# The adaLN gate of a hybrid attention step, moved from TensorE's query stage to VectorE, GpSimd and ScalarE

## Chip, cores, metric

One core of one Trainium2 chip. The metric is the device time of one execution in microseconds (us), the median of several runs. The engines are named as in the profile: PE is TensorE's matmul queue and PEld its weight loads, DVE is VectorE, ACT ScalarE, POOL GpSimd and SP SyncE, which here only issues DMAs. ACTq and SPq rows are DMA issues of those engines.

## What is computed

One layer of a diffusion backbone, over 128 context tokens and 1024 latent tokens of width 1024. Cut to what matters here:

```
shift, scale, gate = split(silu(cond) @ w_mod + b_mod, 3)      # cond = c for latent tokens, c_ctx for context tokens
h  = rmsnorm(x) * (1 + scale) + shift
p  = h @ w_in             # queries, keys, values and SiLU gates of head groups A (global) and B (windowed)
o_a, o_b = attention of each group
x  = x + gate * (concat(o_a * silu(g_a), o_b * silu(g_b)) @ w_out)
```

The adaLN `gate` is two rows of 1024 numbers, one for each kind of token: `silu(c)` and `silu(c_ctx)` times the last third of `w_mod` (1024 x 1024, 4 MB in f32), plus its part of `b_mod`. Nothing needs it before the output projection, near the middle of the kernel.

## The kernel before

Tokens are 9 tiles of 128 (tile 0 is the context), weights are streamed by blocks of 128 rows. Products with f32 accuracy are made of three passes over parts in a rounded format: `Weights.split` makes a high part on ACT and a low part, the difference, on DVE (L233 to L235). The stages follow each other: modulation with the first gate columns, the SiLU gates of group A, **the query stage**, keys and values, the SiLU gates of group B, attention with the output projection.

The query stage (L551 to L675, pool `qt`) sweeps the 9 token tiles twice: m=0 for the queries of group A, m=1 for those of B. Each tile is one `block` (L267) of 24 products into a PSUM bank, written out in two halves. Before each half `tick()` runs what was put on an agenda with `later(n, f)`, n ticks ahead. Within one tick the agenda runs in the order in which it was filled, and at the end `in_order` ties every engine to the order in which the program was written (L1260). So an instruction that waits holds back all that was written after it for its engine.

For block b the agenda of `query` (L586) holds:

- tick 2b+3, `squares`: squares on ACT (sqq), their sums on DVE (ssq, then ms), a power on POOL (rs, L173);
- tick 2b+5, `scale`: on DVE the scaled queries (qn) and the rotary products (ra, then rb in two parts);
- tick 2b+6, `rotated`: their sum on DVE (qf);
- tick 2b+9, `turned`: four transposes on PE (ptq, L622) into one of two PSUM banks used in turn (`bank_tr`), a copy on ACT (qo0, L625) and its store, issued by ACT (L635);
- tick 2b+10, `low`: the remainder on DVE (qo1, L630), stored by ACT one tick later.

A turning bank is free for block b+2 when qo1 of block b has been taken from it. In the last block of a sweep `split` prepares the weights of the next: `W_QB` at the end of m=0, `W_KV` at the end of m=1. Their raw tiles are loaded by `load_all` (L225) before the last block but one, where the second pair of rotary tables (`rope_tables`, L541) is loaded too; DVE multiplies the tables by the norm gains two ticks later (L546).

The gate is computed by PE in the same stage. Its weights come in four loads of 1 MB into two buffers (`load_wg`, L579); for each half of the columns, `gate_rows` (L569) runs 16 products in four groups of rows at once, ACT copies the bank, and `gate_sum` (L563) adds the four groups with a small product of PE and stores the row in DRAM (`gate_row`), from where it is read back, one row repeated over 128 partitions, before attention (L1055).

Of the kernel before, what the change touches and what calls it, by code (L numbers as in the profile page):

```python
# [9 lines left out]
F32 = mybir.dt.float32  # L10
F32R = mybir.dt.float32r
BF16 = mybir.dt.bfloat16
AF = mybir.ActivationFunctionType
ALU = mybir.AluOpType
# [4 lines left out]
P = 128  # L19
D = 1024  # L20
KT = D // P
# [50 lines left out]
EX_AT = (2, 2, 5)  # L72
ROWS_AT = (1, 1, 4, 6)
KV_ORDER = [0] + list(range(1, NT))
GATE_AT = (3, 7)
QUERY_LAST = (0, 1, 2, 4)
CACHE_AT = 8
VC_AT = 6
# [29 lines left out]
def hybrid_step(ctx, tc, x_prompt, x_sample, cache_k_a, cache_v_a, cache_k_b, cache_v_b,  # L108
# [3 lines left out]
    nc = tc.nc  # L112
# [7 lines left out]
    gate_row = dram.tile([2, D], F32, name="gate_row")  # L120
# [5 lines left out]
    def later(n, f):  # L126

        agenda.setdefault(now[0] + n, []).append(f)
# [26 lines left out]
    ident_r = cst.tile([P, P], F32R, name="ident_r")  # L155
# [45 lines left out]
    silc = sm.tile([P, 16], F32, name="silc")  # L201
# [109 lines left out]
    with tc.tile_pool(name="st", bufs=2, side="right") as st:  # L311
# [29 lines left out]
        sil32 = st.tile([P, KT, 32], F32, name="sil32", bufs=1)  # L341
# [99 lines left out]
        for j in range(KT + 2):  # L441
# [42 lines left out]
            if X_FROM + 1 < j <= X_FROM + 4:  # L484
                t = rest[j - X_FROM - 2]
# [8 lines left out]
            if KT - 2 <= j < KT:  # L494
# [3 lines left out]
                c0, n = W_QA.cols[0]  # L498
# [52 lines left out]
    with tc.tile_pool(name="qt", bufs=2, side="right") as qt:  # L551
        for w in (W_QB, W_KV):
            w.pools = [(qt, KT)] * KT


        sil32 = qt.tile([P, KT, 32], F32, name="sil32g", bufs=1)
        nc.gpsimd.memset(sil32, 0.0)
        nc.vector.tensor_copy(sil32[:, :, 0:2], silc.rearrange("p (c k) -> p k c", c=2))
        sel = qt.tile([P, 2], F32, name="selg", bufs=1)
        group_sum(sel, ident_r.bitcast(F32))  # L560
        wg, bg = [], []

        def gate_sum(n, grow):  # L563
            pgs = bank_tr(f"pgs{n}")
            nc.tensor.matmul(pgs[0:2], sel, grow, start=True, stop=True)
            nc.vector.tensor_tensor(bg[n], pgs[0:2], bg[n], op=ALU.add)
            nc.sync.dma_start(gate_row[:, 512 * n : 512 * n + 512], bg[n])

        def gate_rows(n):  # L569
            pg = bank_mm(f"pgate{n}")  # L570
            for k in range(KT):
                a = 32 * (k % 4)
                nc.tensor.matmul(pg[a : a + 32], sil32[:, k, :], wg[2 * n + k // 4][:, k % 4, :],
                                 start=(k < 4), stop=(k >= 4), tile_position=(0, a))
            grow = qt.tile([P, 512], F32, tag="grow", name=f"grow{n}", bufs=1)
            later(1, lambda: nc.scalar.copy(grow, pg))
            later(3, lambda: gate_sum(n, grow))

        def load_wg(i):  # L579
            n, b = divmod(i, 2)  # L580
            wg.append(qt.tile([P, 4, 512], F32, tag="wg", name=f"wg{i}"))
            nc.sync.dma_start(wg[i], w_mod_g[512 * b : 512 * b + 512, 512 * n : 512 * n + 512].rearrange(
                "(k p) n -> p k n", p=P))


        def query(pq, m, t, tabs, n=1):  # L586

            nm = f"q{m}_{t}"
            pqv = pq.rearrange("p (h d) -> p h d", d=HD)
            v = {}  # L590

            def squares():
                sq = qt.tile([P, 8, HD], F32, tag="sq", name=f"sq{nm}")
                nc.scalar.activation(sq, pqv, AF.Square)  # L594
                ss = qt.tile([P, 8], F32, tag="ss", name=f"ss{nm}")
                nc.vector.tensor_reduce(ss, sq, axis=AX.X, op=ALU.add)
                v["r"] = rsqrt_mean(qt, ss, HD, 8, nm)

            def scale():
                qn = qt.tile([P, 8, HD], F32, tag="qn", name=f"qn{nm}")  # L600
                nc.vector.tensor_tensor(qn, pqv, v["r"].unsqueeze(2).to_broadcast([P, 8, HD]), op=ALU.mult)
                v["qn"] = qn
                if t:
                    v["rot"] = rope_products(qt, qn, 8, *tabs[m], t, nm)

            def rotated():

                qf = qt.tile([P, 4, 2, HD], F32, tag="qf", name=f"qf{nm}", bufs=3)
                out = qf.rearrange("p h g d -> p g h d")
                pair = lambda a: a.rearrange("p (g h) d -> p g h d", g=2)  # L610
                if t:
                    nc.vector.tensor_tensor(out, *(pair(a) for a in v["rot"]), op=ALU.add)
                else:
                    nc.vector.tensor_tensor(
                        out, pair(v["qn"]), gain4[:, 2 * m, :].unsqueeze(1).unsqueeze(1).to_broadcast([P, 2, 4, HD]),
                        op=ALU.mult)
                v["qf"] = qf

            def turned():
                ptq = bank_tr(f"pt{nm}")  # L620
                for h in range(4):
                    nc.tensor.transpose(ptq[:, P * h : P * h + P], v["qf"][:, h].rearrange("p g d -> p (g d)"),  # L622
                                        ident_r.bitcast(F32))
                qo = [qt.tile([P, 512], F32R, tag=f"qo{i}", name=f"qo{i}{nm}") for i in range(2)]
                nc.scalar.copy(qo[0], ptq)  # L625
                put(qo[0], 0)
                later(1, lambda: low(ptq, qo))

            def low(ptq, qo):
                nc.vector.tensor_tensor(qo[1], ptq, qo[0], op=ALU.subtract)  # L630
                later(1, lambda: put(qo[1], 1))

            def put(part, i):
                for g in range(2):
                    nc.scalar.dma_start(q_dram[t][m][64 * i : 64 * i + 64, 512 * g : 512 * g + 512],  # L635
                                       part[64 * g : 64 * g + 64].bitcast(F32))

            for d, f in zip(QUERY_LAST if (m, t) == (1, 0) else QUERY_AT, (squares, scale, rotated, turned)):
                later(n + d, f)

        tabs = {0: rope_tables(qt, 0, 2)}
        for m in range(2):
            w, nxt = ((W_QA, W_QB), (W_QB, W_KV))[m]
            ts = list(range(1, NT)) + [0]
            for t in ts:
                pq = bank_mm(f"pq{m}_{t}")
                if m == 1 and t in (ts[GATE_AT[0]], ts[GATE_AT[1]]):
                    gate_rows(len(wg) // 2 - 1)
                if (m, t) in ((0, ts[-2]), (1, ts[GATE_AT[0]])):
                    n = len(wg) // 2  # L650
                    load_wg(2 * n)
                    load_wg(2 * n + 1)
                    if n == 0:
                        bgt = qt.tile([34, 512], F32, name="bg", bufs=1)
                    bg.append(bgt[32 * n : 32 * n + 2])
                    nc.sync.dma_start(bg[n], b_mod[:, 2 * D + 512 * n : 2 * D + 512 * n + 512].to_broadcast([2, 512]))
                if t == ts[-2]:
                    nxt.load_all()
                    if m == 0:
                        tabs[1] = rope_tables(qt, 2, 2)  # L660
                block(pq, lambda k: project(pq, w, t, k), nxt, t == ts[-1])
                query(pq, m, t, tabs)

        kc = gsw4
        vc = wrp.tile([P, 512], F32, tag="raw", name="vc")[:, 0:256].rearrange("p (m g d) -> p m g d", m=2, g=2)
        for m, (ck, cv) in enumerate(((cache_k_a, cache_v_a), (cache_k_b, cache_v_b))):
            nc.sync.dma_start(kc[:, 2 * m : 2 * m + 2, :], ck[0, 0])
            nc.sync.dma_start(vc[:, m], cv[0, 0])
        pks = []
        for t in KV_ORDER[:AHEAD]:  # L670
            pk = bank_mm(f"pk{t}")
            block(pk, lambda k: project(pk, W_KV, t, k), None, False)
            pks.append(pk)
        while agenda:
            tick()  # L675
# [348 lines left out]
    for i in EARLY:  # L1024
        items, end = max_items(i)
# [260 lines left out]
def _layout(c, c_ctx, norm_gain, b_mod, w_mod):  # L1286

    cols = np.concatenate([a.reshape(-1, P) for a in (c, c_ctx, norm_gain, b_mod)]).T
    w = w_mod[0].reshape(KT, P, 3, KT, P)
    ss = np.stack([w[:, :, 1], w[:, :, 0]], axis=2).transpose(3, 1, 0, 2, 4)  # L1290
    return {"cols": cols, "w_mod_ss": ss, "w_mod_g": w_mod[0][:, 2 * D :]}


# [29 lines left out]
```

## Time and profile before

| | |
|---|---|
| median of 3 runs | 723.17 us (723.15 to 726.25) |
| profiled execution | span 721.3 us; its own device time is not listed apart from the three runs, the median of which is 1.9 us above the span |
| PE busy | 698.3 us, 97% of the span |
| DVE, ACT, POOL busy | 457.6 (63%), 411.7 (57%), 335.3 us (46%) |
| mean granted TensorE clock | 0.993 of full speed |
| DMA | 78.56 MB, mean 109 GB/s |
| query stage, m=0 | from 89.3 to 140.8 us |
| query stage, m=1 | from 140.8 to 201.8 us |

How to read it: shares are averages over stages with different limits. A row of a timeline gives start, length, engine, line, operation, output <- inputs and a count; what stands in brackets is how long the engine was idle before it and what it waited for. A row of the groups gives the count, the busy time, the mean ns of one, and the idle time before.

### The profile page before, as it was taken

To read this page: it belongs to the slowest core of one execution; us is meant where nothing else is said; L and a number is where in the kernel's file an instruction comes from. 1 tells how busy PE (TensorE), PEld (TensorE's weight loads), DVE (VectorE), ACT (ScalarE), POOL (GpSimd) and SP (SyncE) were. 2 spreads that over 40 slices of the span, in tenths; PEclk is the share of its full clock that TensorE was granted. 3 is DMA by queue.
4 is the path that set the end of the run, shared out by engine and by line. 5 is a ranking of instruction groups with operands and counts; after the bars stand their busy time and mean duration, and the time that the engine had idled before them with its cause. 6 is when DMAs were issued, how large, how long until landed. Compare 5 with 4: busy or idle time off the path is not lost. (4 is left out here: it accounts for less than half of the span.)

```text
span 721.3 us, 10622 instructions
## 1 busy us (share of the span) xinstructions
PE 698.3 (97%) x3524; PEld 559.7 (78%) x3524; DVE 457.6 (63%) x1007; ACT 411.7 (57%) x829; POOL 335.3 (46%) x355
## 2 busy tenths in 40 slices
PE   5999999999999999999999999999999999999997
PEld 2678988877777788977788888888888888887865
DVE  3466147875675872745866677577666775775653
ACT  5355411411232451158778877877787778877770
POOL 3456013332322340236666555655575557555751
PEclk9999999999999999999999999999999999999999
DMA  8961373348435115440321222121212221212323
GB/s 344 346 219 59 121 278 86 79 94 276 121 85 142 45 60 171 139 143 23 103 67 45 73 67 88 44 81 52 87 54 59 66 87 45 81 53 87 103 65 119
DMA packets 53159, 78.56 MB, mean 109 GB/s; under 512 B 6569, under 2 KB 25449, under 8 KB 52081
## 3 DMA queue, kind: packets, MB, share of 16 engines
q1 hardware_dynamic: 44928, 65.96, 28.1%
q10 hardware_dynamic: 8176, 11.94, 6.3%
q8 instruction: 28, 0.46, 0.3%
q14 instruction: 27, 0.21, 0.1%
HBM read 58.69 MB, written 19.18 MB: 108 GB/s over the span
## 5 line engine op out<-in xcount | busy, mean ns | idle before, releaser
L1108 POOL TENSOR_TENSOR pl<-pe,ph 128x512 fp32r<-128x512 f32 x130 | 167.6, 1292 | 144.7 <-DVE nm L919 67.5
L859 DVE TENSOR_REDUCE mx<-pmx 128x1 f32<-128x384 f32 x192 | 101.4, 552 | 59.5 <-PE pmx L858 58.1
L1100 ACT ACTIVATE pe<-st 128x512 f32<-128x512 f32 x146 | 86.8, 594 | 28.0 <-PE st L1098 27.1
L1104 ACT CAST ph<-pe 128x512 fp32r<-128x512 f32 x146 | 90.6, 621 | 4.8
L1118 PE MATMUL pv<-ph,v_hi 128*128 128x512 f32 x208 | 83.2, 400 | 2.2 <-DVE spare L1142 2.2
L1121 PE MATMUL pv<-pl,v_hi 128*128 128x512 f32 x208 | 82.6, 397 | 0.0
L173 POOL TENSOR_TENSOR rs_q<-ms_q,mhalf 128x8 f32<-128x8 f32 x18 | 34.8, 1931 | 82.1 <-DVE ms_q L171 82.1
L1189 PE MATMUL po<-wo,ogh 128*128 128x512 f32 x216 | 72.5, 394 | 0.2 <-DVE yt L1196 0.2
L919 DVE CUSTOM_DVE_ANT_0 sn<-sn,mask,nsink 128x512 f32<-128x512 f32 (+1 forms) x64 | 46.3, 724 | 38.3 <-PE sn L916 36.5
L858 PE MATMUL pmx<-kha,qt 128*128 128x384 f32 x192 | 61.0, 363 | 0.4 <-ACT pen L905 0.2
L1097 PE MATMUL st<-qt,kha 128*128 128x512 f32 x144 | 58.3, 405 | 1.5 <-ACT pe L1100 0.8
L1098 PE MATMUL st<-qb,kla 68*128 68x512 f32 x144 | 57.6, 400 | 1.1 <-DVE qb L878 1.1
L1120 PE MATMUL pv<-ph,v_lo 128*64 128x512 f32 x146 | 57.9, 396 | 0.0
L1121 PEld LDWEIGHTS pv<-pl,v_hi 128*128 128x128 f32 x208 | 39.4, 189 | 16.7 <-issue 0.2
L905 ACT ACTIVATE pen<-sn,nm 128x512 f32<-128x512 f32 (+2 forms) x72 | 45.0, 626 | 6.5 <-DVE nm L919 3.1
L1093 ACT CAST ph<-st 128x512 fp32r<-128x512 f32 x62 | 36.4, 587 | 19.9 <-PE st L1092 18.7
L1118 PEld LDWEIGHTS pv<-ph,v_hi 128*128 128x128 f32 x208 | 39.4, 189 | 10.5 <-ACT ogh L1154 2.4
L1189 PEld LDWEIGHTS po<-wo,ogh 128*128 128x128 f32 x216 | 40.0, 188 | 6.8 <-DVE yt L1196 0.6
L1094 DVE TENSOR_TENSOR pl<-st,ph 128x512 fp32r<-128x512 f32 x62 | 42.5, 686 | 2.3 <-ACT ph L1093 1.5
L1189 PE MATMUL po<-wo,ogl 128*128 128x512 f32 x108 | 42.6, 394 | 0.0
L594 ACT ACTIVATE sqq<-pq 128x512 f32<-128x512 f32 x18 | 10.8, 599 | 53.3 <-DMA qd<-qo0q 14.4
L858 PEld LDWEIGHTS pmx<-kha,qt 128*128 128x128 f32 x192 | 35.5, 190 | 6.2 <-DVE mx L859 1.4
(216 smaller groups left out, 1700.2 us busy)
## 6 DMA issues: line engine op xcount, KB each, us to landing
qt<-qd SPq DMA_DIRECT2D x36, 256.0 KB, 3.1
wm<-in_w_mod_ss_dram SPq DMA_DIRECT2D x8, 1024.0 KB, 5.1
qd<-qo0q ACTq DMA_DIRECT2D x36, 128.0 KB, 2.4
qd<-qo1q ACTq DMA_DIRECT2D x36, 128.0 KB, 2.4
sgl<-gd SPq DMA_DIRECT2D x36, 128.0 KB, 2.1
out_dram<-yt SPq DMA_DIRECT2D x17, 256.0 KB, 2.1
xn<-in_x_sample_dram SPq DMA_DIRECT2D x8, 512.0 KB, 7.0
wg<-in_w_mod_g_dram SPq DMA_DIRECT2D x4, 1024.0 KB, 7.9
```

The costliest lines, as they stand in the source:

```text
L858: nc.tensor.matmul(pm[:, 0:384], lhs, kha[:, g, 3 * b : 3 * b + 3, :], start=True, stop=True)
L859: nc.vector.tensor_reduce(mx[:, h, b : b + 1], pm[:, 0:384], axis=AX.X, op=ALU.max)
L919: nc.vector.tensor_tensor_reduce(s, s, mask[:, m0 : m0 + n], -1.0, nsink[:, 4 * g + h : 4 * g + h + 1], op0=ALU.add, op1=ALU.min, accum_ou ...
L1097: nc.tensor.matmul(s, kh, qtile[i], start=True, stop=False)
L1098: nc.tensor.matmul(s, kl, qbtile[i], start=False, stop=True)
L1100: nc.scalar.activation(pe, s, AF.Exp)
L1104: nc.scalar.copy(ph, pe)
L1108: nc.gpsimd.tensor_tensor(pl, pe, ph, op=ALU.subtract)
L1118: nc.tensor.matmul(pv, two, ph, start=(b == 0), stop=False)
L1120: nc.tensor.matmul(pv[0:64, :], vl, ph, start=False, stop=False)
L1121: nc.tensor.matmul(pv, two, pl, start=False, stop=last)
L1189: nc.tensor.matmul(po[n], a, wo_parts[KT * n + k][lo], start=(k == KS[0] and p == 0), stop=(k == KS[-1] and p == 2))
```

## The change

The gate's products and sums leave PE. The host hands over the gate's third of `w_mod` transposed, with `c` and `c_ctx` as two more rows. A column of the gate is then a sum along the free dimension: for each of 8 groups of 128 columns a tile of transposed weights (128 x 1024) is multiplied by the SiLU of `c_ctx` on POOL and summed by an accumulating copy on ACT, and multiplied by the SiLU of `c` and summed in one instruction on DVE. The 16 columns get their bias, are turned by one transpose on PE, and go to `gate_row` as before.

The two condition rows are repeated over the partitions (`silb`, 2 x 512 KB written) and loaded at the head of the stage, ahead of the first rotary tables, together with the first two weight tiles. The weights now come in 8 loads of 512 KB through two buffers; each later load follows, one tick on, the sum that frees its buffer. Column group j is begun at tick 6 + 3j (`GATE_AT`), its sums are at the tick after that, the bias at tick 30 and the transpose at tick 31.

```diff
-GATE_AT = (3, 7)
+GATE_AT = (6, 3)
...
-        sil32 = qt.tile([P, KT, 32], F32, name="sil32g", bufs=1)
-        nc.gpsimd.memset(sil32, 0.0)
-        nc.vector.tensor_copy(sil32[:, :, 0:2], silc.rearrange("p (c k) -> p k c", c=2))
-        sel = qt.tile([P, 2], F32, name="selg", bufs=1)
-        group_sum(sel, ident_r.bitcast(F32))
-        wg, bg = [], []
-        def gate_sum(n, grow):
...
-        def gate_rows(n):
...
+        silb = qt.tile([P, 2, D], F32, name="silb", bufs=1)
+        gcol = qt.tile([P, 2, KT], F32, name="gcol", bufs=1)
+        gbias = qt.tile([P, KT], F32, name="gbias", bufs=1)
+        for c in range(2):
+            nc.sync.dma_start(silb[:, c], w_mod_g[D + c : D + c + 1, :].to_broadcast([P, D]))
+        nc.sync.dma_start(gbias, cols[:, 40:48])
+        wg = {}
+        def load_wg(j):
+            wg[j] = qt.tile([P, D], F32, tag="wg", name=f"wg{j}")
+            nc.sync.dma_start(wg[j], w_mod_g[P * j : P * j + P, :])
+        def gate_silu(c):
+            nc.scalar.activation(silb[:, c], silb[:, c], AF.Silu)
+        def gate_columns(j):
+            prod = qt.tile([P, D], F32, tag="prod", name=f"prod{j}", bufs=1)
+            nc.gpsimd.tensor_tensor(prod, wg[j], silb[:, 1], op=ALU.mult)
+            def summed():
+                nc.scalar.activation(prod, prod, AF.Copy, accum_out=gcol[:, 1, j : j + 1])
+                w = wg.pop(j)
+                nc.vector.tensor_tensor_reduce(w, w, silb[:, 0], 1.0, 0.0, op0=ALU.mult, op1=ALU.add,
+                                               accum_out=gcol[:, 0, j : j + 1])
+                if j + 2 < KT:
+                    later(1, lambda: load_wg(j + 2))
+            later(1, summed)
+        def gate_turned():
+            pt = bank_tr("ptg")
+            nc.tensor.transpose(pt[0:16, 0:P], gcol.rearrange("p c j -> p (c j)"), ident_r.bitcast(F32))
+            grow = qt.tile([16, P], F32, name="grow", bufs=1)
+            nc.scalar.copy(grow, pt[0:16, 0:P])
+            nc.sync.dma_start(gate_row.rearrange("c (j n) -> (c j) n", n=P), grow)
+        for j in range(2):
+            load_wg(j)
+            later(3 + j, lambda j=j: gate_silu(j))
+        for j in range(KT):
+            later(GATE_AT[0] + GATE_AT[1] * j, lambda j=j: gate_columns(j))
+        end = GATE_AT[0] + GATE_AT[1] * KT
+        later(end, lambda: nc.vector.tensor_tensor(gcol, gcol, gbias.unsqueeze(1).to_broadcast([P, 2, KT]), op=ALU.add))
+        later(end + 1, gate_turned)
...
-                if m == 1 and t in (ts[GATE_AT[0]], ts[GATE_AT[1]]):
-                    gate_rows(len(wg) // 2 - 1)
-                if (m, t) in ((0, ts[-2]), (1, ts[GATE_AT[0]])):
-                    n = len(wg) // 2
-                    load_wg(2 * n)
-                    load_wg(2 * n + 1)
...
-    return {"cols": cols, "w_mod_ss": ss, "w_mod_g": w_mod[0][:, 2 * D :]}
+    return {"cols": cols, "w_mod_ss": ss, "w_mod_g": np.concatenate([w_mod[0][:, 2 * D :].T, c.reshape(1, D), c_ctx.reshape(1, D)])}
```

More of the change, by code (lines that the diff above doesn't have):

```diff
@@ L553, in hybrid_step @@
             w.pools = [(qt, KT)] * KT
-        sil32 = qt.tile([P, KT, 32], F32, name="sil32g", bufs=1)
-        nc.gpsimd.memset(sil32, 0.0)
-        nc.vector.tensor_copy(sil32[:, :, 0:2], silc.rearrange("p (c k) -> p k c", c=2))
-        sel = qt.tile([P, 2], F32, name="selg", bufs=1)
-        group_sum(sel, ident_r.bitcast(F32))
-        wg, bg = [], []
-        def gate_sum(n, grow):
[L564 to L567, printed above, removed]
@@ L569, in gate_rows @@
-        def gate_rows(n):
[L570 to L583, printed above, removed]
+        silb = qt.tile([P, 2, D], F32, name="silb", bufs=1)
[3 more added lines that the diff above has]
+            nc.sync.dma_start(silb[:, c], w_mod_g[D + c : D + c + 1, :].to_broadcast([P, D]))
@@ L646, in hybrid_step @@
                 pq = bank_mm(f"pq{m}_{t}")
-                if m == 1 and t in (ts[GATE_AT[0]], ts[GATE_AT[1]]):
-                    gate_rows(len(wg) // 2 - 1)
-                if (m, t) in ((0, ts[-2]), (1, ts[GATE_AT[0]])):
-                    n = len(wg) // 2
-                    load_wg(2 * n)
-                    load_wg(2 * n + 1)
[L653 to L656, printed above, removed]
                 if t == ts[-2]:
```

## The prediction

> **What bounds the kernel now.** I read the page first (its slices show TensorE at 90% or more nearly throughout), then the busy time of the two query sweeps (m=0 and m=1), where the change works, then each engine's timeline of a query block, then the DMA issues.
>
> ```profile
> 89.29:141.11 51.82, 51.82 (x241) 42.79 (x241) 34.20 (x74) 11.29 (x22) 14.61 (x9) 1.00 0.49 154
> 141.11:201.70 60.59, 59.87 (x287) 44.45 (x285) 42.95 (x83) 17.11 (x32) 18.52 (x10) 1.00 0.55 152
> ```
>
> After start and end the columns are length, then busy time of PE, PEld, DVE, ACT and POOL. TensorE is never idle in the first sweep and 0.7 us in the second. Whatever leaves its queue here is time gained, and whatever makes it wait is time lost. The gate is here:
>
> ```profile
> 122.96 0.60 PE L622 MATMUL ptq<-ident_r,qfq 128*128 128x128 f32 x4
> 128.89 0.60 PE L622 MATMUL ptq<-ident_r,qfq 128*128 128x128 f32 x4
> ...
> 140.76 0.60 PE L622 MATMUL ptq<-ident_r,qfq 128*128 128x128 f32 x4
> ...
> 147.09 0.60 PE L622 MATMUL ptq<-ident_r,qfq 128*128 128x128 f32 x4
> ...
> 159.05 1.92 PE L573 MATMUL pgate<-wg,sil32g 128*32 128x512 f32 x16
> ...
> 194.61 1.02 PE L565 MATMUL pgs<-grow,selg 128*2 128x512 f32 x2
> ...
> 201.76 0.63 PE L622 MATMUL ptq<-ident_r,qfq 128*128 128x128 f32 x4 [0.47 <-DVE qo1q L630]
> ```
>
> A query block takes 5.93 us (122.96 to 128.89). Nine blocks from 140.76 would end at 194.1, but the second sweep ends at 201.76: 7.6 us more. Of these the two products take 1.9 each, the two sums 1.0 each, the wait for split weights at the sweep's start 0.6 (below), and the rest, 1.2, goes mostly to waits for a turning bank (0.47 of it in the last row), since the sums shift the rotation of the two banks.
>
> **What the change removes.** 3.8 + 2.0 of TensorE and, if nothing takes their place, the 1.2 of bank waits: at most 7.0 us. It adds one transpose, as cheap as two of the four in a 0.60 row: 0.3. The copies and sums taken from the other engines were off the path. So a fully hidden gate would give -6.7.
>
> **What it adds to the others.** Eight times: a 128x1024 product on POOL, an accumulating copy of it on ACT, and a fused product with sum on DVE.
>
> ```profile
> L1108 POOL TENSOR_TENSOR pl<-pe,ph 128x512 fp32r<-128x512 f32 x130 | 167.6, 1292 | 144.7 <-DVE nm L919 67.5 <-ACT ph L1104 56.9 <-POOL pl L1108 10.2
> L1144 POOL TENSOR_TENSOR spare<-spare,sgl 128x256 f32<-128x256 f32 x36 | 26.6, 738 | 3.6 <-DVE spare L1142 2.5 <-POOL ogl L1156 0.6
> ```
>
> ```profile
> L382 ACT ACTIVATE sq<-xn 128x1024 bf16<-128x1024 f32 x9 | 9.5, 1054 | 5.1 <-DMA xn<-in_x_sample_dram 4.8
> L382 ACT ACTIVATION_READ_ACCUMULATOR sq<-xn 128x1 f32 x9 | 1.7, 190 | 0.0
> ```
>
> ```profile
> L919 DVE CUSTOM_DVE_ANT_0 sn<-sn,mask,nsink 128x512 f32<-128x512 f32 x48 | 36.4, 757 | 27.0 <-PE sn L916 26.8 <-ACT pen L905 0.2
> L919 DVE CUSTOM_DVE_ANT_0 sn<-sn,mask,nsink 128x384 f32<-128x384 f32 x16 | 10.0, 624 | 11.3 <-PE sn L916 9.7 <-ACT ph L1104 1.4
> L919 DVE DVE_READ_ACCUMULATOR2_ANT nm<- 128x1 f32 x64 | 8.1, 127 | 0.4
> ```
>
> POOL: 0.55 more per 256 elements, so 1.29 + 2 x 0.55 = 2.4. ACT: 1.24. DVE: 0.133 per 128 elements gives 0.757 + 0.53 = 1.29, and the read 0.13; with the overlap of neighbours I take 1.35. Two SiLUs of 1.05 stand early on ACT, where it is idle.
>
> These stand in the queues of a loop that has little room:
>
> ```profile
> 128.01 0.17 DVE L171 TENSOR_SCALAR ms_q<-ssq 128x8 f32<-128x8 f32 x1
> 128.09 0.69 DVE L612 TENSOR_TENSOR qfq<-ra_q,rb_q 128x512 f32<-128x512 f32 x1
> 128.69 0.68 DVE L630 TENSOR_TENSOR qo1q<-ptq,qo0q 128x512 fp32r<-128x512 f32 x1
> 130.30 0.69 DVE L601 TENSOR_TENSOR qnq<-pq,rs_q 128x512 f32<-128x512 f32 x1 [0.93 <-POOL rs_q L173]
> 131.03 0.69 DVE L531 TENSOR_TENSOR ra_q<-qnq,tcos 128x512 f32<-128x512 f32 x1
> 131.64 0.75 DVE L537 TENSOR_TENSOR rb_q<-qnq,tsin 128x256 f32<-128x256 f32 x2
> 133.22 0.69 DVE L596 TENSOR_REDUCE ssq<-sqq 128x8 f32<-128x512 f32 x1 [0.83 <-ACT sqq L594]
> ```
>
> ```profile
> 106.81 2.02 POOL L173 TENSOR_TENSOR rs_q<-ms_q,mhalf 128x8 f32<-128x8 f32 x1 [3.00 <-DVE ms_q L171]
> ...
> 128.32 1.94 POOL L173 TENSOR_TENSOR rs_q<-ms_q,mhalf 128x8 f32<-128x8 f32 x1 [3.99 <-DVE ms_q L171]
> ```
>
> ```profile
> 130.15 1.10 ACTq L635 DMA_DIRECT2D qd<-qo0q  x2
> 131.34 1.20 ACTq L635 DMA_DIRECT2D qd<-qo1q  x2
> 132.59 0.60 ACT L594 ACTIVATE sqq<-pq 128x512 f32<-128x512 f32 x1 [2.47 <-DVE rb_q L537]
> ```
>
> From the power's end (130.26) to the next sum of squares could be 2.05 us, and from there to the next power's end 2.97 (0.71, 0.3 and 1.94): 5.0 against TensorE's 5.93. The product needs only its weights, so POOL begins it as soon as a power ends, just when DVE goes on to the two rotary products. What the two do to each other:
>
> ```profile
> 258.26 2.99 POOL L235 TENSOR_TENSOR wlogb<-rawgb,whigb 128x512 fp32r<-128x512 f32 x2 [1.42 <-ACT whigb L233]
> ```
>
> ```profile
> 260.26 1.54 DVE L235 TENSOR_TENSOR wlogb<-rawgb,whigb 128x512 fp32r<-128x512 f32 x1 [0.15 <-ACT whigb L233]
> ```
>
> DVE's subtraction of two SBUF tiles, 0.69 in its free form (ra above), ends 0.55 after POOL's (261.25), as if it had begun only then. So ra waits for the product's end: 2.4 + 1.3 = 3.7 from the power's end instead of 2.05.
>
> With GATE_AT = (6, 3) products alternate between two places. **Even ticks:** ACT's accumulating copy waits for the product, with the issue of the qo1 store and the next squares behind it: 2.4 + 1.3 + 1.2 + 0.65 = 5.6 from the power's end to the sum of squares, and 8.55 for the block. **Odd ticks:** rb ends at 3.7, and DVE's fused product stands between qf and qo1, ahead of the next qn: two blocks take 12.05 instead of 10. Three blocks: 20.6, where TensorE takes 17.8. DVE falls behind by 2.8 per three blocks. Its lead is about 5.5: qo1 of 128.69 ends at 129.37, and its bank is turned into again at 134.8.
>
> **What it moves.** On SP, the tables and the next weights:
>
> ```profile
> 92.87 0.34 SPq L545 DMA_DIRECT2D tcos<-in_k_cos_dram  x1
> ...
> 97.88 7.55 SPq L221 DMA_DIRECT2D rawqb<-in_w_in_dram  x8
> ...
> 160.17 1.24 SPq L582 DMA_DIRECT2D wg<-in_w_mod_g_dram  x2
> ```
>
> ```profile
> DMA to landing us min/median/max: 7.9/7.9/7.9
> ```
>
> ```profile
> 99.99 0.68 DVE L546 TENSOR_TENSOR tcos<-tcos,gain 128x512 f32<-128x512 f32 x1
> ...
> 134.62 0.69 DVE L546 TENSOR_TENSOR tcos<-tcos,gain 128x512 f32<-128x512 f32 x1
> ```
>
> Two loads of 1 MB land 7.9 us after issue, some 1.8 of it latency: about 345 GB/s. First, 2 MB now stand ahead of the first tables, which land at about 102 instead of before 100: DVE begins 1.4 late. Second, the fifth weight load reuses the buffer of the third, so SP waits at tick 14 for the fused product of tick 13, and behind it stand the eight loads of the next weights (97.88 before) and the second tables. With the fifth load itself that is 3.1 MB, 9.1 us at that rate, and 1.8: the tables land 10.9 after the wait ends. DVE wants them at 134.62, and everything behind them in its order waits too.
>
> **The walk**, with these lengths, in us from the span's start. Tables 1.4 late: power 1, which ended at 108.8, ends at 110.2.
> Product 0 runs to 112.7, ra and rb to 114.0, the fused product to 115.4, and power 2 ends at 115.4 + 2.97 = 118.4.
> Product 1 to 120.8, rb to 122.1; sum of squares, qf, fused product and qo1 of block 0 follow in DVE's order (0.7, 0.7, 1.35, 0.6): 125.45. TensorE turns block 2 into block 0's bank and was due at 122.96: **2.5**. Power 4 ends at 118.35 + 12.05 = 130.4.
> Product 2 (even): fused product to 130.4 + 3.7 + 1.35 = 135.5, sum of squares at 130.4 + 5.6 = 136.0, then qf and qo1 of block 2 to 138.0. TensorE is due at 125.45 + 2 x 5.93 = 137.3: **0.7**. SP, free at 135.5, gets the second tables at 146.4.
> Power 5 ends at 139.0, product 3 at 141.4, rb at 142.7, qf at 144.1. Here DVE stands for the tables until 146; their two products, the fused product and qo1 of block 3 take it to 149.1. TensorE was due at 144.0: **5.1**.
>
> ```profile
> 139.96 1.29 DVE L235 TENSOR_TENSOR wloqb<-rawqb,whiqb 128x512 fp32r<-128x512 f32 x2
> ...
> 143.11 0.19 PEld L249 LDWEIGHTS pq<-wloqb,h 128*128 128x128 f32 x1 [0.56 <-DVE wloqb L235]
> ```
>
> The split of the next weights, started at 139.96 and costing TensorE 0.6, now follows the scaling of block 6 and the squares of block 7: it starts at 151.9. Power 7 ends at 154.05 and product 4 follows, to 156.5; the third part of the split, also of two SBUF tiles, waits for it and is there at 157.1. From there TensorE needs 4.0 to the block's end as before (143.11 to 147.1): 161.1, where 149.1 + 5.93 was due: **6.1**.
> In m=1 three blocks again take 20.6, so the lead won by these waits is used up. At tick 31 the added transpose takes block 9's bank (qo1 at 192.3) and pushes block 11 onto block 10's, whose qo1 comes one tick before (196.3); TensorE was due at 161.1 + 5 x 5.93 = 190.8: **5.5**. Then no products are left and DVE gains 0.9 a block.
>
> ```profile
> 171.47 9.84 SPq L221 DMA_DIRECT2D rawkv<-in_w_in_dram  x16
> ```
>
> ```profile
> 199.11 1.30 DVE L235 TENSOR_TENSOR wlokv<-rawkv,whikv 128x512 fp32r<-128x512 f32 x2
> ```
>
> The key weights, issued at 171.5, now stand behind the gate's store of tick 31, so from about 197 to 207. Their split, 5.1 after the turn that stands just ahead of the second sum (194.0 before, 208.2 now), comes at 213: covered by some 3 us, and each us beyond that would be lost whole.
> Sum: 2.5 + 0.7 + 5.1 + 6.1 + 5.5 = 19.9 of waits, less the 7.6 that goes (the old wait for the split is inside the 6.1), plus 0.3: **+12.6**. The later stages keep their order and shift whole. The span becomes 721.3 + 12.6 = 733.9; the page gives this execution no other time, and the median of the runs, 723.17, lies 1.9 above the span: **735.8**.
>
> **The rivals.** *All hidden:* if DVE keeps its 5.5 us lead (the product overlaps the rotary products freely, ACT's order does not bind, and loads come in time), the gain stays: 723.2 - 6.7 = 716.5. For it: POOL and ACT are under a third busy in both sweeps. Against it: the 1.54 row. It decides while three blocks take less than 17.8.
> *Only the late loads bind:* fused product 2 ends at 127.8, tables at 138.7 against 134.62, 4.1 lost at the split: 723.2 + 4.1 - 6.7 = 720.6, no change that can be told (0.5%, 3.6 us, is about the least that can).
> *Slowed, not blocked:* if ra and rb merely stretch, odd pairs lose 1.7 less. The same walk then loses 0.7 at tick 17, 3.5 at the fourth turn, 4.8 at the split and 3.4 at the end, 12.4 in all: +5, 728. The 1.54 row speaks against it. [...]
> [...]
>
> **How the numbers follow.** Forecast 0.45, half rate 0.10, slowed only 0.15: slower 0.70. Late loads alone 0.13: the same. All hidden 0.17: faster. The range leaves out all hidden and little above half rate: 719.5 to 745. The signs are not balanced, so one range stands.
>
> **What would show it.** Rotary products of about 2.5 us beside POOL's product; ACT's square behind the accumulating copy; blocks of 20 us in threes; rawqb issued after 128, with DVE waiting for tcos; TensorE idle before ptq (from qo1) and before wloqb. Wrong, if the fused product's rows lie in DVE's idle time and ptq never waits: then the gain is kept. Wrong too if rawqb goes out early.

## The result: 2.5% slower, and the profile after

| | before | after |
|---|---|---|
| median of 4 runs each | 723.16 us | 741.06 us (740.75 to 741.98) |
| ratio | 1 | 1.0249, 95% interval 1.0232 to 1.0266 |
| span of the profiled execution | 721.3 us | 739.0 us |
| PE busy | 698.3 us | 695.5 us |

The forecast was 735.8 (719.5 to 745), slower with 0.70. Sign and range held; the growth was 17.7 us of span where 12.6 were forecast. The page after:

```profile
PE 695.5 (94%) x3489; PEld 560.3 (76%) x3489; DVE 476.2 (64%) x1018; ACT 420.9 (57%) x846; POOL 354.2 (48%) x362
...
PEclk9999999959999999999999999999999999999999
```

TensorE does what was intended: 35 matmuls fewer. It is no faster for it, since it now waits, and one slice, the ninth, shows a TensorE clock of half speed. The two query sweeps after (length, then busy PE, PEld, DVE, ACT, POOL; then clock, DMA share, GB/s):

```profile
88.35:150.50 62.15, 52.18 (x237) 42.10 (x236) 38.24 (x67) 14.30 (x26) 22.96 (x11) 0.97 0.46 150
150.50:219.50 69.00, 60.66 (x264) 47.94 (x264) 56.92 (x100) 24.13 (x45) 29.05 (x14) 0.91 0.47 130
```

PE, idle for 0.7 us in the two sweeps before, is now idle for 18 us in them (10.0 and 8.3; the boundary at 150.50 lies inside its longest wait). Its timeline after, at the turns and wherever it waited:

```profile
118.12 0.65 PE L638 MATMUL ptq<-ident_r,qfq 128*128 128x128 f32 x4 [1.51 <-DVE qfq L628]
126.38 0.66 PE L638 MATMUL ptq<-ident_r,qfq 128*128 128x128 f32 x4 [2.13 <-DVE qo1q L646]
...
138.29 0.60 PE L638 MATMUL ptq<-ident_r,qfq 128*128 128x128 f32 x4
152.54 1.11 PE L638 MATMUL ptq<-ident_r,qfq 128*128 128x128 f32 x4 [8.15 <-DVE qo1q L646]
154.82 0.80 PE L248 MATMUL pq<-whiqb,h 128*128 128x512 f32 x1 [1.17 <-ACT whiqb L233]
155.94 0.79 PE L249 MATMUL pq<-wloqb,h 128*128 128x512 f32 x1 [0.32 <-DVE wloqb L235]
160.33 0.80 PE L249 MATMUL pq<-wloqb,h 128*128 128x512 f32 x1 [1.47 <-DVE wloqb L235]
165.78 0.60 PE L638 MATMUL ptq<-ident_r,qfq 128*128 128x128 f32 x4
...
196.94 0.27 PE L588 MATMUL ptg<-ident_r,gcol 128*16 128x128 f32 x1 [1.33 <-DVE gcol L599]
198.05 0.66 PE L638 MATMUL ptq<-ident_r,qfq 128*128 128x128 f32 x4 [0.84 <-DVE qo1q L646]
...
217.89 0.50 PE L249 MATMUL pk<-wlokv,h 128*128 128x512 f32 x1 [1.17 <-DVE wlokv L235]
220.30 0.50 PE L249 MATMUL pk<-wlokv,h 128*128 128x512 f32 x1 [0.74 <-DVE wlokv L235]
224.29 0.60 PE L638 MATMUL ptq<-ident_r,qfq 128*128 128x128 f32 x4
```

Against the pace of 5.93 us a block, the turn of 118.12 is 1.7 late, that of 126.38 another 2.3, that of 152.54 another 8.3; the block that splits the second weights (152.54 to 165.78) takes 7.3 too much, the one with the gate's transpose (to 198.05) 2.6, and the one that splits the key weights (to 224.29) 2.5. That is 24.7 us of new losses against the 7.6 that went: 17.1. The first turn came 0.6 earlier than before, and 1.2 more are lost at the first turns of the keys and behind; otherwise the later stages shift whole.

The cause of most waits is in DVE's rows:

```profile
102.84 0.69 DVE L546 TENSOR_TENSOR tcos<-tcos,gain 128x512 f32<-128x512 f32 x1 [3.11 <-DMA tcos<-in_k_cos_dram]
...
112.67 2.19 DVE L531 TENSOR_TENSOR ra_q<-qnq,tcos 128x512 f32<-128x512 f32 x1
...
115.44 1.21 DVE L579 CUSTOM_DVE_ANT_0 wg<-wg,silb 128x1024 f32<-128x1024 f32 x1
...
116.59 0.67 DVE L612 TENSOR_REDUCE ssq<-sqq 128x8 f32<-128x512 f32 x1
...
126.95 0.69 DVE L531 TENSOR_TENSOR ra_q<-qnq,tcos 128x512 f32<-128x512 f32 x1
...
135.89 0.68 DVE L612 TENSOR_REDUCE ssq<-sqq 128x8 f32<-128x512 f32 x1
...
149.08 0.69 DVE L546 TENSOR_TENSOR tcos<-tcos,gain 128x512 f32<-128x512 f32 x1 [5.21 <-DMA tcos<-in_k_cos_dram]
...
157.62 2.66 DVE L235 TENSOR_TENSOR wloqb<-rawqb,whiqb 128x512 fp32r<-128x512 f32 x1
```

```profile
111.88 2.42 POOL L574 TENSOR_TENSOR prod<-wg,silb 128x1024 f32<-128x1024 f32 x1
```

The rotary product ra takes 0.69 alone (126.95) and 2.19 beside POOL's product, whose end at 114.30 it outlasts by 0.56. A part of the weights' split, also of two SBUF tiles, does the same at 157.62: it takes 2.66, where the median of the eight parts is 0.68, and ends 0.55 after the product that ran from 157.35 to 159.73. So both end as if they had begun when the product ended. In what follows this is called the lock. The grouped rows of the stage show it for all sixteen ra together, before and then after (count, busy, mean ns of one, idle before):

```profile
L531 DVE TENSOR_TENSOR ra_q<-qnq,tcos 128x512 f32<-128x512 f32 x16 | 11.1, 693 | 0.5
```

```profile
L531 DVE TENSOR_TENSOR ra_q<-qnq,tcos 128x512 f32<-128x512 f32 x16 | 20.0, 1252 | 0.5
L579 DVE CUSTOM_DVE_ANT_0 wg<-wg,silb 128x1024 f32<-128x1024 f32 x8 | 9.7, 1218 | 0.0
...
L574 POOL TENSOR_TENSOR prod<-wg,silb 128x1024 f32<-128x1024 f32 x8 | 19.3, 2417 | 0.0
```

Of the sixteen, six stood behind a product: 8.9 us more in all, 1.5 each. Three blocks of DVE's loop, with one product on an even and one on an odd tick, take 19.3 us (the sums of squares of 116.59 and 135.89), where TensorE needs 17.8.

The second cause is SP's queue:

```profile
116.69 19.63 SPq L566 DMA_DIRECT2D wg<-in_w_mod_g_dram  x3
136.37 7.31 SPq L221 DMA_DIRECT2D rawqb<-in_w_in_dram  x8
143.73 0.54 SPq L545 DMA_DIRECT2D tcos<-in_k_cos_dram  x1
```

SP stands with the last of these three, the fifth gate load, until the fused product of 134.75 has left its buffer at 135.97, and is free at 136.3; the second weights and tables, issued from 97.88 on before, follow only then, and DVE stands idle for 5.21 us before the tables (149.08).

### The profile page after: what moved, and what is told of

Same layout as the page of the kernel before. It is cut to its first block, busy times and chain, and to the rows that moved or that the text cites. A ratio compares the mean times of both kernels' runs of the same rounds, so it can differ in the third digit from the quotient of the medians.

```text
span 739.0 us, 10612 instructions
## 1 busy us (share of the span) xinstructions
PE 695.5 (94%) x3489; PEld 560.3 (76%) x3489; DVE 476.2 (64%) x1018; ACT 420.9 (57%) x846; POOL 354.2 (48%) x362
## 5 line engine op out<-in xcount | busy, mean ns | idle before, releaser
L1099 ACT CAST ph<-st 128x512 fp32r<-128x512 f32 x62 | 36.4, 587 | 19.9 <-PE st L1098 18.7
L407 POOL TENSOR_TENSOR h<-hf,h 128x256 fp32r<-128x256 f32 (+2 forms) x32 | 28.3, 902 | 22.6 <-DVE h L406 22.6
```

## The experiments

Three things could make the loss: the lock that POOL's product holds against ra, the loads behind the gate's buffers, and the plain amount of work on DVE and ACT. The rival theories were that one of the last two carries it. Each run is given with its ratio to runs of before that were made beside it, the medians of which lie between 722.45 and 723.24 us; the differences to after are differences of medians, and can be off by as much.

**e1: second weights and tables at the head of the stage.**

```diff
         tabs = {0: rope_tables(qt, 0, 2)}
+        W_QB.load_all()
+        tabs[1] = rope_tables(qt, 2, 16)
...
-                if t == ts[-2]:
+                if t == ts[-2] and m == 1:
                     nxt.load_all()
-                    if m == 0:
-                        tabs[1] = rope_tables(qt, 2, 2)
```

> Of the change alone, the loads of the second weights and tables go back to the head of the stage (before any weight of the gate that must wait for a buffer). In-order theory: DVE's wait of 5.2 us for tcos is gone, TensorE's wait before the fourth turn falls from 8.15 to about 3 us, the granted clock stays 1.0, and as DVE is what TensorE waits for at tick 31, the whole end moves by DVE's 5.2: about 736 us. Capacity theory (DVE has simply 10 us more to do and 12 us of blocking): the order of loads does not matter, 740 to 741.

737.67 us, ratio 1.0199 (1.0181 to 1.0217): 3.4 below after, between the 736 and the 740 of the two theories. The wait of 8.15 shrinks to 1.04, where 3 were expected, but the next block takes 11.8, since DVE is still behind when the split comes. Late tables were not the bound by themselves: most of what they cost, the lock takes anyway. In this execution TensorE's clock halved at another place, after a shorter wait:

```profile
127.63 1.07 PE L638 MATMUL ptq<-ident_r,qfq 128*128 128x128 f32 x4 [2.13 <-DVE qo1q L646]
```

```profile
127.60:131.50 3.90, 3.87 (x12) 3.25 (x13) 3.83 (x8) 1.07 (x2) 0.98 (x1) 0.56 0.79 232
```

**e2: TensorE kept busy through the long wait.** 34 products of no use stand before the turn of 152.54.

```diff
+                if (m, t) == (1, ts[0]):
+                    for _ in range(34):
+                        nc.tensor.matmul(pq, ident_b, ident_b.unsqueeze(1).to_broadcast([P, 4, P]), start=True, stop=True)
                 block(pq, lambda k: project(pq, w, t, k), nxt, t == ts[-1])
```

> The change with 34 idle products put into TensorE's queue ahead of the fourth turn, where it waits 8.15 us (34 x 0.23 = 7.7 us fit in). They leave all else alone. If the halved clock behind that wait costs time of its own: the block behind it ends 1.6 us sooner, 739.5 us. If DVE is what binds at tick 31, the 1.6 us are waited for there: 741 us, with the clock at 1.0 throughout.

740.43 us, ratio 1.0243 (1.0221 to 1.0265): not told apart from after (its runs go from 739.81 to 742.80, those of after from 740.75 to 741.98). The run decides between neither of the two forecasts, since the clock, at 1.00 through the wait, was halved in three other places: behind the turns of 126.86 and 198.04 (0.56 over 127.60 to 131.50 and 0.67 over 198.00 to 202.00; blocks of 7.6, which took 6.0 in after) and in the block of the split itself (0.81 over 158.00 to 164.00), where products take 0.63 from 161.83 to 165 and about 0.4 otherwise:

```profile
160.31 0.50 PE L249 MATMUL pq<-wloqb,h 128*128 128x512 f32 x1 [2.76 <-DVE wloqb L235]
...
161.83 0.63 PE L249 MATMUL pq<-wloqb,h 128*128 128x512 f32 x1
```

It does show that DVE sets the pace here. The turn behind that of 126.86 is 2.1 later than in after, but TensorE's last wait for the split ends at 160.31, as in after (160.33). From there to the next turn it takes 5.6 here and 5.45 in after, both with products of 0.63 for some 3 us, and 4.0 in e1 with products of 0.40 (156.05 to 160.08): about 1.4 us of after's block is the halved clock. Whether they reach the end of the kernel no run shows; the 1.6 lost behind 126.86 here do not.

**e3: without the context row's half.** POOL's product and ACT's sum go.

```diff
-            prod = qt.tile([P, D], F32, tag="prod", name=f"prod{j}", bufs=1)
-            nc.gpsimd.tensor_tensor(prod, wg[j], silb[:, 1], op=ALU.mult)
...
-                nc.scalar.activation(prod, prod, AF.Copy, accum_out=gcol[:, 1, j : j + 1])
+                if j == 0:
+                    nc.vector.tensor_copy(gcol[:, 1, :], gbias)
```

> The change without POOL's product and ACT's sum: the context tokens' gate is left out (the bias stands in its place). No lock, only DVE's 8 fused products. Three blocks take 16.6 us on DVE against TensorE's 17.8, so DVE keeps pace but for the late tables: fused product 2 ends at 128.5, the tables come 13 us later as in the change (141.5), DVE is 6 us late at the split: about 724 us. If the fused products themselves saturate DVE: 731 us or more.

730.70 us, ratio 1.0111 (1.0083 to 1.0138): 10.4 below after, all sixteen ra at 692 ns. The 724 of the expectation was missed on the high side. It had counted 6 us for the late tables; the turn that waits for them is 6.2 late, the block of the split behind it takes 5.1 too much, and the one that splits the key weights 2.6. That turn:

```profile
147.54 1.12 PE L638 MATMUL ptq<-ident_r,qfq 128*128 128x128 f32 x4 [6.07 <-DVE qo1q L646]
```

**e4: without the latent row's half.** The eight fused products on DVE go.

```diff
                 w = wg.pop(j)
-                nc.vector.tensor_tensor_reduce(w, w, silb[:, 0], 1.0, 0.0, op0=ALU.mult, op1=ALU.add,
-                                               accum_out=gcol[:, 0, j : j + 1])
+                if j == 0:
+                    nc.vector.tensor_copy(gcol[:, 0, :], gbias)
```

> The change without DVE's fused products: the latent tokens' gate is left out (the bias stands in its place). The lock and ACT's sums stay. Three blocks take 18.9 us on DVE: 1.1 behind per three blocks, and the tables still come late (about 144.5): 733 to 737 us. If the fused products were the cause and the lock nothing: 718 to 720 us.

739.90 us, ratio 1.0238 (1.0210 to 1.0266): 1.2 below after, and 0.7 of that lies in the runs of before beside it (722.45 instead of 723.16); the 733 to 737 of the theory were missed, and the 718 to 720 of its rival far more. The two halves read the same weights and hold the same numbers of products, but POOL's half, with ACT's sums, is worth 10.4 and DVE's, which takes 10.3 us of DVE itself, 1.2 at most. The amount of work on DVE was not the cause.

**e5: ACT's sum a tick later where it stood before the squares.**

```diff
+            later(1 + (j + 1) % 2, lambda: nc.scalar.activation(prod, prod, AF.Copy, accum_out=gcol[:, 1, j : j + 1]))
...
             def summed():
-                nc.scalar.activation(prod, prod, AF.Copy, accum_out=gcol[:, 1, j : j + 1])
```

> The change with ACT's sums of the even places one tick later, behind the squares instead of ahead of them. The prediction's 5.6 us (ACT's order binds on even places): 3 x 0.9 us less by the split, about 738 us. DVE's own order binds (ra waits for the lock, then the fused product): no change, 741 us.

742.36 us, ratio 1.0269 (1.0238 to 1.0301): nothing gained, as the second theory had it. On even places the sum of squares comes 4.7 after the power's end with or without ACT's sum ahead of the squares (131.20 to 135.89 in after, 132.20 to 136.89 here): DVE's order sets it, ra held to the product's end, rb and the fused product, not ACT's.

**e6 and e7: halves.** Sixteen half products, one every second tick, so that the lock is only half as long; e7 also loads early, as e1.

```diff
-GATE_AT = (6, 3)
+GATE_AT = (4, 2)
...
+            j, h = divmod(i, 2)
+            hs = slice(512 * h, 512 * h + 512)
+            prod = qt.tile([P, 512], F32, tag="prod", name=f"prod{i}", bufs=2)
+            nc.gpsimd.tensor_tensor(prod, wg[j][:, hs], silb[:, 1, hs], op=ALU.mult)
+            w = wg[j][:, hs]
+            nc.vector.tensor_tensor_reduce(w, w, silb[:, 0, hs], 1.0, 0.0, op0=ALU.mult, op1=ALU.add,
+                                           accum_out=ghalf[:, h, 0, j : j + 1])
+            later(2, lambda: nc.scalar.activation(prod, prod, AF.Copy, accum_out=ghalf[:, h, 1, j : j + 1]))
```

> The same work for the gate in 16 halves of 512, one to a block: POOL's product right after the power as before, but half as long; DVE's fused product in the even tick, where DVE waits for the power; ACT's sum in an even tick. In-order theory: ra waits only 0.55 us for the lock, DVE's loop is 5.0 + 0.6 = 5.6 us against TensorE's 5.93, no turn waits, and the 6 to 7 us taken from TensorE are kept: 717 to 719 us. Capacity theory (the engines have no room for this work in the stage): DVE's sum of work is even a little larger, so 738 us or more.

> The halves with the loads of the second weights and tables at the head of the stage. In-order theory: 717 to 719 us, at most 1 us from the halves alone, since there the tables come when DVE is about to need them. Capacity theory: 738 us or more.

762.88 us, ratio 1.0546 (1.0520 to 1.0571), and 762.20, ratio 1.0545 (1.0519 to 1.0572): far on the other side. The number lies where the capacity theory put it, but the cause is another. POOL and then DVE of e7:

```profile
133.93 1.64 POOL L173 TENSOR_TENSOR rs_q<-ms_q,mhalf 128x8 f32<-128x8 f32 x1 [4.88 <-DVE ms_q L171]
135.53 1.30 POOL L577 TENSOR_TENSOR prod<-wg,silb 128x512 f32<-128x512 f32 x1
```

```profile
136.87 0.69 DVE L579 CUSTOM_DVE_ANT_0 wg<-wg,silb 128x512 f32<-128x512 f32 x1 [3.08 <-POOL prod L577]
```

The fused product writes over the weights that it reads, and POOL reads the same half. In after it stands a tick behind the product, which is long done; here it was issued in the same tick, so it waits 3.08 us in block after block, and qf, qo1 and the next qn behind it. The cycle is 7.78 (the powers of 126.14, 133.93 and 141.72).

**e8: e7 with a scratch tile for the output.**

```diff
-            nc.vector.tensor_tensor_reduce(w, w, silb[:, 0, hs], 1.0, 0.0, op0=ALU.mult, op1=ALU.add,
+            spare = qt.tile([P, 512], F32, tag="sparep", name=f"sparep{i}", bufs=1)
+            nc.vector.tensor_tensor_reduce(spare, wg[j][:, hs], silb[:, 0, hs], 1.0, 0.0, op0=ALU.mult, op1=ALU.add,
```

> The kernel of e7 (products in halves every other tick, second weights and tables loaded at the head of the stage), but the fused product writes a scratch tile instead of the weights it reads, so it no longer waits for GpSimd's product of the same half. Theory (the miss of e6 and e7 was that wait, 3.08 us in every block of e7's trace; half a product holds a rotary product back by only some 0.6 us): DVE's cycle falls from 7.78 to 5.6 or 5.8, below TensorE's 5.93, and the time is 718 to 724. Rival (sixteen products on GpSimd are too many for a cycle whatever the order, since its power and its product take turns): about 760, as e7.

729.80 us, ratio 1.0097 (1.0080 to 1.0114): 32 below e7 by the output's place alone. DVE's cycle falls to 5.37, below TensorE's 5.93, and ra is held by 0.36 (1.05 instead of 0.69), to 0.54 after the end of the half product (124.37):

```profile
123.14 0.69 DVE L617 TENSOR_TENSOR qnq<-pq,rs_q 128x512 f32<-128x512 f32 x1 [0.32 <-POOL rs_q L173]
123.86 1.05 DVE L531 TENSOR_TENSOR ra_q<-qnq,tcos 128x512 f32<-128x512 f32 x1
...
128.51 0.69 DVE L617 TENSOR_TENSOR qnq<-pq,rs_q 128x512 f32<-128x512 f32 x1 [0.32 <-POOL rs_q L173]
```

The time still misses the 718 to 724. TensorE waits 3.1 us for wloqb and whiqb, and that block takes 3.9 too much (141.24 to 151.12). More is lost where the split of the key weights and the gate's transpose meet: the turn behind that of 198.59 comes at 212.76, 8.2 too late, with waits of 1.4, 0.8, 2.0 and 1.5, all for DVE, and a stretch with products of 0.63 instead of about 0.4 in between, as at the clock of 0.50 in after.

**e9: both rows on DVE alone.** Sixteen whole fused products, one every second tick from tick 4, into a scratch tile; nothing on POOL and ACT.

```diff
+            j, c = divmod(i, 2)
+            prod = qt.tile([P, D], F32, tag="prod", name=f"prod{i}", bufs=1)
+            nc.vector.tensor_tensor_reduce(prod, wg[j], silb[:, c], 1.0, 0.0, op0=ALU.mult, op1=ALU.add,
+                                           accum_out=gcol[:, c, j : j + 1])
```

> After, but GpSimd and ScalarE have no part in the gate: both rows of all eight column groups are fused products on VectorE, 16 of 128x1024, one at every second tick from tick 4 (where VectorE has the power of GpSimd to wait for), into a scratch tile. That is twice the work on VectorE (16 x 1.29 = 20.6 us instead of 10.3), none on the other two, and no load of weights waits for a late buffer. Theory (the loss is the lock that GpSimd's product holds against the rotary products, and the loads that queue behind it): all of it hides, the time is 723.2 - 6.7 = 716.5, up to 719. Rival (VectorE's capacity is the limit): three blocks take 15 + 3 x 1.3 = 18.9 us or more against 17.8, some 6 us lost over the stage and later split of the weights, 729 to 741.

727.10 us, ratio 1.0054 (1.0039 to 1.0069): 14.0 below after, with twice the gate's work on DVE, and between the forecasts (716.5 to 719, 729 to 741). A version without the lock is faster although the engine that it held does more. It is not the lock alone that goes: ACT's sums go with it, and the buffers come free earlier, so that the second weights are issued at 123.19 instead of 136.37. e3 and e11 part these: 10.4 for the lock with ACT's sums, 6.5 for the loads. What ACT's sums cost by themselves was tested on even places only (e5: nothing). POOL and DVE in one block:

```profile
127.33 2.48 POOL L173 TENSOR_TENSOR rs_q<-ms_q,mhalf 128x8 f32<-128x8 f32 x1 [3.07 <-DVE ms_q L171]
```

```profile
127.10 1.22 DVE L575 CUSTOM_DVE_ANT_0 prod<-wg,silb 128x1024 f32<-128x1024 f32 x1
...
129.84 0.69 DVE L611 TENSOR_TENSOR qnq<-pq,rs_q 128x512 f32<-128x512 f32 x1 [0.31 <-POOL rs_q L173]
```

Here the power is the one that is held: 1.94 behind the shorter qf in before, it takes 2.48 and ends 1.49 after the fused product's end (128.32). But most of the product lies in the time that DVE waited for the power, and a block takes 5.54. What is left of the loss is at the split of the second weights, where TensorE waits 3.5 us and the block takes 6.8 too much, and at the gate's transpose (2.0).

**e10: e9 with the first tables ahead of the gate's loads.**

```diff
+        tabs = {0: rope_tables(qt, 0, 2)}
         silb = qt.tile([P, 2, D], F32, name="silb", bufs=1)
...
-        tabs = {0: rope_tables(qt, 0, 2)}
```

> The kernel of e9 with the first rotary tables loaded ahead of the gate's condition rows and weights, as in the kernel before. Theory (the late first tables cost the turn of the second and third block some 1 to 2 us, as in after's trace): 1 to 2 us below e9. Rival (VectorE makes the late start good before any turn is due): the same as e9 within 0.5 us.

728.48 us (725.57 to 729.66), ratio 1.0067 (1.0044 to 1.0090): not told apart from e9, so that neither the 1 to 2 us of the theory nor the 0.5 of the rival is shown. Its stage did end earlier (the last turns at 213.5 instead of 216.1), but its four runs spread over 4 us.

**e11: after, with all its loads out of the way.** First tables first, second weights and tables at the third block, key weights one block earlier; POOL's products as in after.

```diff
-                if t == ts[-2]:
-                    nxt.load_all()
-                    if m == 0:
-                        tabs[1] = rope_tables(qt, 2, 2)
+                if m == 0 and t == ts[2]:
+                    nxt.load_all()
+                    tabs[1] = rope_tables(qt, 2, 12)
+                if m == 1 and t == ts[-3]:
+                    nxt.load_all()
```

> After with all loads out of the way of the gate's buffers: first tables ahead of the gate's loads, second weights and tables issued at the third block (before any load of gate weights has to wait), weights of keys and values one block earlier (before the gate's store). The lock stays: whole products on GpSimd, sums on ScalarE. Theory (loads and lock each carry a part; the lock alone makes three blocks 20.6 us against 17.8 and shifts the rotation of the turning banks): 730 to 736. Rival (only the loads mattered): 716 to 720. Rival (the loads did not matter, as the small gain of loading at the head of the stage suggests): 738 to 741.

734.59 us, ratio 1.0164 (1.0138 to 1.0191): 6.5 below after and inside the 730 to 736 of the theory: the lock with ACT's half remains, and is worth more than the loads (10.4 in e3). The wait for tables is gone; in its place TensorE waits 2.48 at the same turn and 3.84 at the gate's transpose, both for DVE.

**e12: e10 with the products kept away from the split.**

```diff
-GATE_AT = (4, 2)
+GATE_AT = (4, 6, 8, 10, 20, 22, 23, 24, 26, 27, 28, 30, 31, 32, 33, 34)
...
-        later(end + 1, gate_turned)
+        later(end + 5, gate_turned)
...
-                if t == ts[-2]:
+                if t == ts[-2] and m == 0:
                     nxt.load_all()
-                    if m == 0:
-                        tabs[1] = rope_tables(qt, 2, 2)
+                    tabs[1] = rope_tables(qt, 2, 2)
+                if t == ts[1] and m == 1:
+                    nxt.load_all()
```

> The kernel of e10, but with no fused product between tick 10 and tick 20, so that none stands ahead of the split of the second weights (in e10's trace that split ends at 150.0 instead of 149.6 - 3.6 = 146.0 before, and TensorE waits 2.8 us in three places for it); the twelve later ones go to ticks 20 to 34, the weights of keys and values are loaded at the second sweep's second block, ahead of the gate's buffers, and the gate's transpose comes five ticks after its sums, behind the last turn of the stage, where it shifts no bank of the turns. Theory (with the lock gone, what is left in e9 and e10 is the place: the split, 2.8, and the gate's transpose with the turn behind it, 2.7): 723.2 - 6.7 = 716.5, up to 720. Rival (VectorE's capacity in the second sweep, where the fused products now stand closer: 12 in 14 ticks, 12 x 1.3 = 15.6 us in seven blocks of 5.93 in which its cycle without them is 5.0 to 5.14, so 35 + 15.6 = 50.6 against 41.5, less the 2 or so that lie in waits and a lead of 5.5): 2 us or so lost at the end of the stage, 719 to 724.

722.03 us (12 runs) against 722.99 (17 runs), ratio 0.9984 (0.9972 to 0.9996): the fastest of all, a microsecond below before, too little to count as faster. The rival's 719 to 724 holds. Where the other six went, in PE's timeline:

```profile
144.02 0.50 PE L249 MATMUL pq<-wloqb,h 128*128 128x512 f32 x1 [0.75 <-DVE wloqb L235]
...
195.50 0.60 PE L633 MATMUL ptq<-ident_r,qfq 128*128 128x128 f32 x4
197.24 0.50 PE L249 MATMUL pk<-wlokv,h 128*128 128x512 f32 x1 [0.90 <-DVE wlokv L235]
199.73 0.50 PE L249 MATMUL pk<-wlokv,h 128*128 128x512 f32 x1 [0.84 <-DVE wlokv L235]
203.71 0.60 PE L633 MATMUL ptq<-ident_r,qfq 128*128 128x128 f32 x4
...
227.82 0.66 PE L728 MATMUL ptk<-ident_r,k2k 128*128 128x128 f32 x4 [2.94 <-ACT k2k L722]
```

At 195.50 this version is 6.3 ahead of before, whose fifteenth turn came at 201.76; 1.0 of it was there at the first turn (110.08 against 111.09), and the rest is the gain. The split of the key weights gives 2.3 back (203.71 against 207.72), the first turn of the keys more, since ACT is late for it (2.94 of waiting, 1.17 before): 227.82 against 229.47. Only 1.7 reach the end of the span (719.6 against 721.3).

## Why the prediction was right, and where its sizes were off

The step that decided the sign held: POOL's product holds ra to its end. Its measured length, 2.42, was the 2.4 of the forecast, and so was the 0.55 behind it. The traces show it in both directions: ra at 2.19 beside the product (after) and the power at 2.48 beside the fused product (e9). "Slowed, not blocked" falls by the same rows. "Late loads alone" falls by e11, in which loads out of the way leave 1.6%; "all hidden" by the waits.

The terms of the sum, forecast and then measured:

- *Turn of block 2*, 2.5: 4.0, as 1.7 at the turn before it (for qf, which the prediction did not walk) and 2.3 here. The first tables, forecast 1.4 late, were 2.85 late (102.84, 99.99 before), and TensorE's own first turn was 0.6 early.
- *Tick 17*, 0.7: nothing. The even place took 7.66 from one sum of squares to the next, not 8.55. The step that failed is that ACT's order binds there: the issue of the qo1 store, which the forecast put behind ACT's sum at 1.2, ran beside it in after (issued at 133.65, the sum at 133.64), and e5 shows that DVE's order sets the 4.7.
- *The turn that waits for the second tables*, 5.1: 8.3. SP was free at 136.4, as forecast within 1 us, but issuing the eight weight loads took 7.31 of its time; the tables were issued at 143.73 and were there at 149.08, 12.7 after the wait's end and not 10.9. (The sum itself took 146 for its 146.4 here: with these the term is 5.5.) The 1.8 of latency and the 345 GB/s of the forecast are estimates; in before a load of 64 KB landed in 1.7 us, and the fullest slices of the page moved 344 and 346 GB/s.
- *The split*, 6.1: 7.3. Its third part waited for product 4, as forecast (the row of 157.62), and was there 7.7 after the turn instead of 8.0. But from there TensorE needed 5.45 and not 4.0, for the halved clock (0.50 over 152.50 to 162.00), which the prediction had not foreseen.
- *Tick 31*, 5.5: 2.6. TensorE had lost 19.6 by then, not 14.4, so DVE was less far behind.
- *The key weights*, "covered by some 3 us": 2.5 lost. They were issued at 198.31 to 208.8, nearly as forecast, but the query stores queue behind them, and ACT with its next squares and high parts behind the stores:

```profile
202.68 0.60 ACT L610 ACTIVATE sqq<-pq 128x512 f32<-128x512 f32 x1 [3.35 <-DMA qd<-qo0q]
...
210.70 0.60 ACT L610 ACTIVATE sqq<-pq 128x512 f32<-128x512 f32 x1 [5.46 <-DMA qd<-qo0q]
...
215.09 4.25 ACT L233 CAST whikv<-rawkv 128x512 fp32r<-128x512 f32 x8
```

The high parts, at 198.17 before, came at 215.09, 16.9 later, where the turn just ahead of the second split part (215.89, 201.76 before) is 14.1 later. Four terms were too small and two too large; the sum of them, 19.9 against 24.7, hides some of the error, and it is in part luck that it lies no further off.

The half rate of the fused product, with its chance of 0.10 and its part in the upper end of the range, no run shows: 1024 elements took 1.22 in after and the read 0.08, 1.30 against the 1.35 of the forecast.

What stays open: how much of the loss is the clock. It was halved at different places in executions of nearly the same order (e1, e2), and the four runs of e10 lie 4 us apart at mean clocks of 0.983 to 0.992.

## What to carry to other kernels

Work moved to an idle engine is paid for where it holds up a busy one: see from the trace what the two engines do to each other side by side before counting idle shares, since here 19 us of products on an engine under a third busy held back the one that TensorE waits for, and giving that one twice the work instead, which also let the loads go earlier, was 14 us cheaper. A load whose buffer is freed by new work can hold back the loads queued after it, so walk the whole queue and not only the buffer: here SP stood up to 18.1 us for one buffer, and the second weights were issued at 136.37 instead of 97.88. And look where time taken off the bounding engine in a stage is given back: of the 6.3 us that e12 was ahead at 195.50, 1.7 reached the end, and the rest went where the others had to catch up, at the split of the key weights and the first turn of the keys.

## What the runs showed of the hardware

The granted clock of TensorE fell to half in or behind some waits and did not return with the work, here in after:

```profile
144.40:152.50 8.10, 0.00 (x0) 0.00 (x0) 3.15 (x6) 0.00 (x0) 0.97 (x1) 0.62 0.52 178
152.50:162.00 9.50, 6.50 (x15) 4.21 (x16) 9.43 (x14) 6.97 (x13) 4.30 (x2) 0.50 0.44 125
162.00:164.00 2.00, 2.00 (x7) 1.56 (x7) 1.97 (x5) 0.00 (x0) 0.00 (x0) 0.64 0.28 64
```

It stayed at 0.50 for 9.5 us after the work had resumed, with 6.5 us of that busy, and was higher again, at 0.64, only in the first stretch without waits (the last of them ended at 160.33). How long a wait has to be for this the runs do not show: in after it fell within a wait of 8.15, and in e1 and e2 a wait of 2.13 was followed by 0.56 over 3.9 us, but in after the same wait of 2.13 by 1.00 (126.00 to 129.90).
